# A squared-ReLU MLP whose second pass over W_down opens with the last pair, then takes the last but one by seven products

## The chip, the cores and the metric

The kernel runs on one core of one Trainium2 chip. The metric is the device time of one execution in microseconds (us): the median of three runs of the kernel before is 2126.35 us (2126.24 to 2127.57). One more execution was taken with the hardware profiler; all rows shown are from it.

## The reference, cut to what matters

Two layers, each a mixer (attention and a gated short convolution, one shared output projection) followed by an MLP. Everything is float32, x has 256 rows and 2048 columns, and the MLP is 8192 wide:

```python
D_MODEL = 2048
SEQ = 256
DEPTH = 2
D_FF = 4 * D_MODEL
...
        hm = _rmsnorm(x, mlp_norm_g[l]) @ w_up[l]
        x = x + jnp.square(jax.nn.relu(hm)) @ w_down[l]
```

The change touches only the second of these lines, the product with W_down (8192 x 2048).

## The kernel before, in words

**Float32 by three products.** Every operand is split into a rounded part ("h", "hi") and the rest ("l", "lo"). One product of two operands is three matmuls (`TERMS`): hi with hi, hi with lo, lo with hi. The rounding to hi is ScalarE's (ACT) work, the subtraction for lo VectorE's (DVE). TensorE (PE) does the matmuls, each 128x128 weights against 128x512 moving values here. In the MLP the activations are PE's weights and the rows of W_down the moving side.

**Pairs.** The width of 8192 is cut into `NP` = 32 pairs, numbered 0 to 31, of 256 hidden columns each: pair i is 256 columns of W_up and the 256 rows of W_down that they meet. A pair against one half (1024 columns) of W_down is a 2x2 by 2x2 block product. Done in the ordinary way it is 8 block products, 24 matmuls (`OWN`, line 1354 in the second pass, line 1267 in the first). Done "by seven" it is Strassen's scheme in Winograd's form: 7 block products, 21 matmuls (helper `product`, line 1177).

**Forms.** Seven products need sums on both sides. Those of the activations (`S1` to `S4`) are made once per pair by `square`; a pair's hi and lo of the eight blocks A21, A11, A22, A12, S1 to S4 are one tile `f` (helper `rounded`). Those of the W_down rows are made per pair and half by `quarters` in three jobs: `plain` (the blocks b1 and b2: b1h, b1l, b2h, b2l), `sums` (t[0:2] at line 1019, then t13h, t13l, then t[2] at line 1022 and t[3] at line 1023) and `more` (t24h, t24l). The seven products use them in that order: products 1, 2, 3 from b1 and b2, then 5 and 7 from t13, then 6 and 4 from t24. Ordinary rows only need hi and lo (`whi`, line 325, and `wlo`, line 326; two halves per pair).

**Two passes.** The first pass runs over pairs 0 to 31: it makes a pair's activations from W_up (the matmuls of `upc`, line 1128) and, two pairs later (`LAG`), multiplies them with the left half of W_down; pairs 0 to 30 by seven, pair 31 in the ordinary way. The sums of the left half lie in eight banks of PSUM (tiles `pr`), and are drained into x at the pass's end by one ACT and eight DVE instructions of 128x512 (lines 1237 and 1232). The second pass multiplies all pairs with the right half (banks `rt`), in an order of its own, written out by hand:

```python
ORDER = tuple(i % NP for i in range(NP - LAG, 2 * NP - LAG))
SEVEN = ORDER[3:NP - LAG:2]
ORDINARY = tuple(i for i in ORDER if i not in SEVEN)
PLAIN = ORDINARY[LAG:]
```

So before, the order is 30, 31, 0, 1, 2, ... 29. Pairs 30 and 31 still have their tiles `f` in SBUF; they come first and in the ordinary way. Of the others, the odd ones from 1 to 27 go by seven; their tiles were stored in DRAM (`whole`) during the first pass and are fetched again by `load_again` on the POOL queue, 896 KB each, two turns ahead. The even ones, 28 and 29 go in the ordinary way and are fetched as `g` from `plain`, two pairs to a block. Rows of W_down come on the SP queue: for pairs by seven into one of three rooms named `draw`, for ordinary pairs into one of three buffers `raw`.

**What sets the order.** PE's instructions stand in the order in which the program writes them. ACT and DVE instructions are placed by a scheduler with a time model of its own, within limits that the code sets (`late` keeps an instruction in program order, `behind` puts it after another); each engine then executes its list strictly in that order. Which weight job is made after which is the list `made_in`, with the table `slots` that says behind which ordinary half the three jobs of a pair by seven are written; a job is written at most three (`AHEAD`) ahead of its use. hi and lo of ordinary rows have three buffers each, so a `whi` waits until PE has finished the half three before it.

Of the kernel before, what the change touches and what calls it, by code (L numbers as in the profile page):

```python
# [10 lines left out]
F32R = mybir.dt.float32r  # L11
# [4 lines left out]
P = 128  # L16
# [16 lines left out]
AHEAD = 3  # L33
NP = DFF // (2 * P)
LAG = 2
ORDER = tuple(i % NP for i in range(NP - LAG, 2 * NP - LAG))
SEVEN = ORDER[3:NP - LAG:2]
ORDINARY = tuple(i for i in ORDER if i not in SEVEN)
PLAIN = ORDINARY[LAG:]

OUT_JOBS = D // P // 2 * (D // CH)
EARLY_UP = {(0, 0): 15, (0, 1): 17, (1, 0): 23}
# [70 lines left out]
def trunk(ctx: ExitStack, tc: tile.TileContext, x, w_in, w_out, conv_w, q_norm_g, k_norm_g,  # L113
# [10 lines left out]
    dram = ctx.enter_context(tc.tile_pool(name="dram", bufs=1, space=bass.MemoryType.DRAM))  # L124
# [808 lines left out]
    def mlp(l, mnorm, ahead, last):  # L933
# [3 lines left out]
        with ExitStack() as scope:  # L937
            upool = scope.enter_context(tc.tile_pool(name="upool", bufs=3))
            fpool = scope.enter_context(tc.tile_pool(name="fpool", bufs=2))
# [16 lines left out]
            raws, forms, units_made, drains = {}, {}, [], []  # L956
# [22 lines left out]
            def load_rows(i, col):  # L979
                raw = (upool.tile([P, 2, 2 * CH], F32, tag="uraw", name="raw") if col and i not in SEVEN else  # L980
                       tile_of("draw", [P, 2, 2 * CH], F32, (first, "draw"), (second, "draw1"),
# [7 lines left out]
            def quarters(i, col=0):  # L989


                keep = late if i == SEVEN[0] and col else lambda ins: None

# [78 lines left out]

            whole = {i: dram.tile([P, 2, 7, P], F32R, name=f"whole{l}_{i}") for i in SEVEN}
            plain = [dram.tile([P, 2, 2, 4, P], F32R, name=f"plain{l}_{b}")
                     for b in range(len(PLAIN) // 2)]
            again, unit_loads = {}, []
# [3 lines left out]
                    unit_loads.append(nc.gpsimd.dma_start(dst, src))  # L1082

            def load_again(i):
                again[i] = fpool.tile([P, 2, 8, P], F32R, tag="f", name="f")
                load_unit(again[i][:, :, 1:], whole[i])

            base = len(weights.jobs)
            where = {}
            for i in ORDER:  # L1090
                where[i] = len(weights.jobs)
                if i in SEVEN:
                    weights.jobs += quarters(i, 2 * CH)
# [5 lines left out]
            mine = [where[i] + k for i in ORDINARY for k in range(2)]  # L1099
            slots = {}  # L1100
            for i in SEVEN:
                before = [j for j in mine if j < where[i]][-4:] if i != SEVEN[0] else [
                    mine[0], mine[1], mine[4]]
                js = [where[i] + k for k in range(3)]
                if len(before) == 4 and SEVEN.index(i) and where[SEVEN[SEVEN.index(i) - 1]] > before[0]:
                    before = [before[2], before[2], before[3]]
                for j, b in zip(js, before):
                    slots.setdefault(b, []).append(j)
# [32 lines left out]
            def square(i, h):  # L1141


                u = h[:, 0:4].rearrange("p a c -> p (a c)")
                nc.scalar.activation(u, u, AF.Relu)
                top = h[:, 0:4].rearrange("p (k t) c -> p k t c", t=2)[:, :, 0]
                nc.vector.tensor_mul(top, top,
                                     mnorm.ratio.unsqueeze(1).to_broadcast([P, 2, P]))
                nc.scalar.activation(u, u, AF.Square)
                if i < NP - 1:  # L1150
                    nc.vector.tensor_add(h[:, S1], h[:, A21], h[:, A22])
                    nc.vector.tensor_sub(h[:, S2], h[:, S1], h[:, A11])
                    nc.vector.tensor_sub(h[:, S3], h[:, A11], h[:, A21])
                    nc.vector.tensor_sub(h[:, S4], h[:, A12], h[:, S2])
                if i in SEVEN:
                    f = rounded(h, 1, 8)
                    nc.gpsimd.dma_start(whole[i], f[:, :, 1:])
                    return f
                f = rounded(h, 0, 8 if i < NP - 1 else 4)
                if i in PLAIN:  # L1160
                    b = PLAIN.index(i)
                    stored.append(nc.gpsimd.dma_start(plain[b // 2][:, b % 2], f[:, :, :4]))
                return f

            def rounded(h, lo, hi):
                f = fpool.tile([P, 2, 8, P], F32R, tag="f", name="f")
                units_made.append((
                    nc.scalar.activation(f[:, 0, lo:hi], h[:, lo:hi], AF.Copy),
                    nc.vector.tensor_sub(f[:, 1, lo:hi], h[:, lo:hi], f[:, 0, lo:hi].bitcast(F32))))
                return f  # L1170
# [9 lines left out]
            fs = {}  # L1180
# [66 lines left out]
            f = fs[NP - 2]  # L1247
# [15 lines left out]
            for k in range(2):  # L1263
                b = weights.take()
# [24 lines left out]
            for n in (5, 4, 8):  # L1289
                prods[n] = bank(f"rt{l}{n}")  # L1290
            for i in ORDER:
                if i in SEVEN:
                    f = again[i]
                    one, end = i == SEVEN[0], i == SEVEN[-1]
                    if one:
                        w2 = mm.tile([P, 2, CH], F32, tag="mm2", name=f"rt{l}1")
                        prods[1], prods[6] = w2[:, 0], w2[:, 1]
                        prods[7] = ps.tile([P, CH], F32, tag="av", name=f"rt{l}7", bufs=1)
                    b11, b21, b22 = weights.take()
                    product(1, f, A11, b11, one, end)  # L1300
                    product(2, f, A12, b21, False)
                    product(3, f, S4, b22, False)
                    work.tick()
                    t1, t3 = weights.take()
                    product(5, f, S1, t1, one, end)
                    product(7, f, S3, t3, one, end)
                    work.tick()
                    t2, t4 = weights.take()
                    product(6, f, S2, t2, one, end)
                    product(4, f, A22, t4, False)  # L1310
                    work.tick()
                    if end:
                        for dst, v in shared(*right):
                            nc.vector.tensor_add(dst, dst, v)
                        if not last:
                            spare = (prods[7], prods[5])
                            work.start(norm.chunk(0, 2, spare), 2)
                            work.start(norm.chunk(1, 2, spare), 6)
                    continue
                n = ORDINARY.index(i)  # L1320
                if NP // 2 - 6 <= n and sums:
                    finish_left()
                if 0 < n <= len(SEVEN):
                    load_again(SEVEN[n - 1])
                b, slot = divmod(n - LAG, 2)
                if b < 0:
                    own = lambda k, t, pa: fs[i][:, pa, 2 * k + t]
                else:
# [3 lines left out]
                    if slot == 1 and b + 2 < len(plain):  # L1332
                        block(b + 2)
                if i == ORDER[-1]:
                    both = [weights.take() for k in range(2)]
# [14 lines left out]
                for k in range(2):  # L1350
                    w = weights.take()
                    for n, t, p in OWN:
                        for m, (pa, pw) in enumerate(TERMS):
                            nc.tensor.matmul(  # L1354
                                prods[p], own(k, t, pa), w[pw][:, n],
                                start=(i == ORDER[0] and k == 0 and m == 0), stop=False)
                        if t:
# [47 lines left out]
```

## Time and profile before

| what | value |
|---|---|
| median of three runs | 2126.35 us |
| the profiled execution | 2126.2 us, its span 2124.1 us |
| PE busy | 2118.3 us of the span |
| DVE busy | 1738.9 us |
| ACT busy | 1299.0 us |
| granted TensorE clock | 1.0 |
| HBM traffic | 234 GB/s over the span |

The span is what the profiler's records cover; the 2.1 us that the execution is longer lie around it. Matmuls overlap in the records: one is shown as about 0.39 us long, and the next begins before it ends. How long PE takes for each is read from the starts. An answer of the timeline gives the start in us, the length in us, the engine, the line, the operation, the tiles and, in brackets, how long the engine had been idle and what released it; "x2" is two instructions in one row. Layer 0's first pass ends and its second begins at 899.69 us of the span, layer 1's at 1954.93 us.

### The profile page before, as it was taken

Reading aid. Unit: us, or ns where it says so; the run is one execution under the profiler, and the core shown is the slowest. Engines: PE = TensorE matmul, PEld = TensorE weight load, DVE = VectorE, ACT = ScalarE, POOL = GpSimd, SP = SyncE. Lnnn points to the kernel's source line nnn. Section 1 sums busy time; section 2 is a strip of 40 time slices with the busy share of each in tenths; the row PEclk is TensorE's granted clock in tenths of the full one; section 3 lists DMA queues with packets and bytes.
Section 4 is the critical chain, followed back from the end, with each engine's and each line's share of the span. In section 5 each row is a group of like instructions: output and inputs, shape, how many; then the busy total and the mean of one; then the engine's idle time right before and its main releaser. Section 6 shows DMA issues by size and latency. Waiting matters only on the chain.

```text
span 2124.1 us, 28896 instructions
## 1 busy us (share of the span) xinstructions
PE 2118.3 (100%) x10926; PEld 1804.4 (85%) x10926; DVE 1738.9 (82%) x2397; ACT 1299.0 (61%) x1775; POOL 188.7 (9%) x282
## 2 busy tenths in 40 slices
PE   9999999999999999999999999999999999999999
PEld 7888888888888888888888888888888888888887
DVE  6677688788888888899866776887888888888897
ACT  6556456666666666655565664566666666666553
POOL 3021200000000000011011221000000000000110
PEclk9999999999999999999999999999999999999999
DMA  8655567687787777699666556677778778776994
GB/s 262 188 165 162 186 210 249 207 251 242 244 244 243 244 245 242 222 360 345 219 215 178 158 163 194 213 247 220 238 246 250 235 245 249 237 245 212 385 359 156
DMA packets 293322, 497.99 MB, mean 234 GB/s; under 512 B 10723, under 2 KB 191541, under 8 KB 293184
## 3 DMA queue, kind: packets, MB, share of 16 engines
q1 hardware_dynamic: 263056, 406.88, 60.1%
q0 software_dynamic: 30080, 89.26, 13.0%
q8 instruction: 85, 1.39, 0.3%
q14 instruction: 53, 0.43, 0.1%
q10 hardware_dynamic: 48, 0.02, 0.0%
HBM read 451.53 MB, written 44.59 MB: 234 GB/s over the span
## 4 chain that ended last, share of the span: by engine, by line
PE 99%; DVE 0%; DMA 0%; ACT 0%; issue 0%
PE upc L1128 31%; PE pr L1177 14%; PE rt L1354 8%; PE rt L1177 6%; PE ci L479 4%; PE gc L479 4%; PE gb L479 4%; PE k L457 4%; PE v L457 4%; PE q L457 4%; PE o L457 4%; PE o L875 3%; PE o L893 1%; PE upw L1128 1%; PE up L1128 1%; PE sc L654 1%
## 5 line engine op out<-in xcount | busy, mean ns | idle before, releaser
L325 ACT ACTIVATE whi<-raw 128x1024 fp32r<-128x1024 f32 x308 | 326.4, 1060 | 411.7 <-PE rt L1354 137.5
L326 DVE TENSOR_TENSOR wlo<-raw,whi 128x1024 fp32r<-128x1024 f32 x308 | 379.5, 1234 | 196.1 <-ACT whi L325 191.1
L1128 PE MATMUL upc<-nT,uhi 128*128 128x512 f32 x1920 | 477.6, 391 | 0.0
L974 ACT ACTIVATE uhi<-uraw 128x1024 fp32r<-128x1024 f32 x256 | 270.4, 1057 | 261.5 <-PE upc L1128 237.3
L1128 PEld LDWEIGHTS upc<-nT,uhi 128*128 128x128 f32 x1920 | 352.9, 188 | 68.0
L975 DVE TENSOR_TENSOR ulo<-uraw,uhi 128x1024 fp32r<-128x1024 f32 x256 | 313.1, 1223 | 118.6 <-ACT uhi L974 109.4
L1128 PEld LDWEIGHTS upc<-nT,ulo 128*128 128x128 f32 x1920 | 262.0, 191 | 18.7
L1128 PE MATMUL upc<-nT,ulo 128*128 128x256 f32 x1920 | 267.8, 283 | 0.0
L1354 PE MATMUL rt<-whi,g 128*128 128x512 f32 x480 | 153.0, 389 | 0.0
L1002 DVE TENSOR_TENSOR t13l<-t,t13h 128x1024 fp32r<-128x1024 f32 x90 | 110.0, 1222 | 2.1
L1019 DVE TENSOR_TENSOR t<-draw 128x1024 f32<-128x1024 f32 x90 | 109.8, 1220 | 0.8
L1002 DVE TENSOR_TENSOR b2l<-draw,b2h 128x1024 fp32r<-128x1024 f32 x90 | 109.6, 1218 | 0.4 <-ACT b2h L1000 0.4
L1002 DVE TENSOR_TENSOR t24l<-t,t24h 128x1024 fp32r<-128x1024 f32 x90 | 109.6, 1218 | 0.0
L1354 PEld LDWEIGHTS rt<-whi,g 128*128 128x128 f32 x480 | 90.1, 188 | 18.6
L1000 ACT ACTIVATE t13h<-t 128x1024 fp32r<-128x1024 f32 x90 | 95.8, 1064 | 3.3 <-PE rt L1177 0.6
L1177 PE MATMUL pr<-t13h,f 128*128 128x512 f32 x248 | 96.6, 391 | 0.0
L1000 ACT ACTIVATE t24h<-t 128x1024 fp32r<-128x1024 f32 x90 | 94.5, 1050 | 1.0 <-DVE t L1023 1.0
L1000 ACT ACTIVATE b2h<-draw 128x1024 fp32r<-128x1024 f32 x90 | 94.5, 1050 | 0.9 <-PE pr L1177 0.8
L1354 PE MATMUL rt<-wlo,g 128*128 128x512 f32 x240 | 93.4, 389 | 0.0
L1177 PE MATMUL pr<-b2h,f 128*128 128x512 f32 x248 | 86.8, 391 | 0.0
L1177 PE MATMUL pr<-t24h,f 128*128 128x512 f32 x248 | 86.8, 391 | 0.0
L457 PE MATMUL k<-whi,nT 128*128 128x512 f32 x256 | 86.1, 400 | 0.0
(414 smaller groups left out, 4086.7 us busy)
## 6 DMA issues: line engine op xcount, KB each, us to landing
uraw<-in_w_up_dram SPq DMA_DIRECT2D x128, 1024.0 KB, 5.9
raw<-in_w_in_dram SPq DMA_DIRECT2D x190, 512.0 KB, 3.9
draw<-in_w_down_dram SPq DMA_DIRECT2D x92, 1024.0 KB, 6.5
raw<-in_w_down_dram SPq DMA_DIRECT2D x36, 1024.0 KB, 8.1
raw<-in_w_out_dram SPq DMA_DIRECT2D x52, 512.0 KB, 4.7
whole<-f POOLq DMA_DIRECT2D x28, 896.0 KB, 4.5
f<-whole POOLq DMA_DIRECT2D x28, 896.0 KB, 8.7
plain<-f POOLq DMA_DIRECT2D x32, 512.0 KB, 3.8
```

Of the source, the lines that this page charges most:

```text
L325: self.splits.append((nc.scalar.activation(hi, raw, AF.Copy), nc.vector.tensor_sub(lo, raw, hi.bitcast(F32))))
L326: nc.vector.tensor_sub(lo, raw, hi.bitcast(F32))))
L457: nc.tensor.matmul(acc[:, t], a.ap[:, pa, k % KG, t * P:(t + 1) * P], (hi, lo)[pw][:, j], start=(k == 0 and n == 0), stop=(k == nk - 1 and ...
L479: nc.tensor.matmul(acc[:, f, 0] if part else acc[:, f], wt[:, k % 4, fs], a.ap[:, 0, k % KG] if part else a.ap[:, :, k % KG], start=(part ...
L974: nc.scalar.activation(hi, src, AF.Copy)
L975: nc.vector.tensor_sub(lo, src, hi.bitcast(F32))
L1000: keep(nc.scalar.activation(hi, src, AF.Copy))
L1002: keep(nc.vector.tensor_sub(lo, src, hi.bitcast(F32)))
L1019: keep(nc.vector.tensor_sub(t[:, 0:2], raw[:, :, 1], raw[:, 0]))
L1128: nc.tensor.matmul(acc[:, 0] if part else acc, wt[:, k], a.ap[:, 0, k % KG] if part else a.ap[:, :, k % KG], start=(part == 0 and kh == 0 ...
L1177: nc.tensor.matmul(prods[n], f[:, pa, a], b[pw], start=(start and m == 0), stop=(stop and m == 2))
L1354: nc.tensor.matmul(prods[p], own(k, t, pa), w[pw][:, n], start=(i == ORDER[0] and k == 0 and m == 0), stop=False)
```

## The change

The second pass's order becomes 31, 30, 0, 1, 2, ... 29. Pair 31 stays ordinary. Pair 30 becomes the first of the pairs by seven, and its products read the tile `f` that is still in SBUF (`fs[i]`), so it isn't stored in DRAM or fetched. The table `slots` gives pair 30's three jobs their places: the first two behind pair 31's first half, the third behind its second (before, pair 1 was the first by seven, with its jobs behind pair 30's first and second half and pair 0's first). The two buffers of tiles `f`, before one rotating tag "f", become two tags "f0" and "f1" that are taken in turns by a count of the pairs, and `load_again` is called for pairs 1 and 3 at pair 0 and then one per ordinary pair.

```diff
@@ -33,10 +33,10 @@
-ORDER = tuple(i % NP for i in range(NP - LAG, 2 * NP - LAG))
-SEVEN = ORDER[3:NP - LAG:2]
+ORDER = (NP - 1, NP - 2, *range(NP - 2))
+SEVEN = ORDER[1:NP - LAG:2]
 ORDINARY = tuple(i for i in ORDER if i not in SEVEN)
-PLAIN = ORDINARY[LAG:]
+PLAIN = ORDINARY[1:]
@@ -1072,7 +1072,7 @@
-            whole = {i: dram.tile([P, 2, 7, P], F32R, name=f"whole{l}_{i}") for i in SEVEN}
+            whole = {i: dram.tile([P, 2, 7, P], F32R, name=f"whole{l}_{i}") for i in SEVEN[1:]}
@@ -1082,7 +1082,7 @@
             def load_again(i):
-                again[i] = fpool.tile([P, 2, 8, P], F32R, tag="f", name="f")
+                again[i] = fpool.tile([P, 2, 8, P], F32R, tag=f"f{SEVEN.index(i) % 2}", name="f", bufs=1)
                 load_unit(again[i][:, :, 1:], whole[i])
@@ -1100,7 +1100,7 @@
             for i in SEVEN:
                 before = [j for j in mine if j < where[i]][-4:] if i != SEVEN[0] else [
-                    mine[0], mine[1], mine[4]]
+                    mine[0], mine[0], mine[1]]
@@ -1152,7 +1152,7 @@
-                if i in SEVEN:
+                if i in SEVEN[1:]:
                     f = rounded(h, 1, 8)
                     nc.gpsimd.dma_start(whole[i], f[:, :, 1:])
                     return f
@@ -1163,7 +1163,7 @@
             def rounded(h, lo, hi):
-                f = fpool.tile([P, 2, 8, P], F32R, tag="f", name="f")
+                f = fpool.tile([P, 2, 8, P], F32R, tag=f"f{len(units_made) % 2}", name="f", bufs=1)
@@ -1290,7 +1290,7 @@
                 if i in SEVEN:
-                    f = again[i]
+                    f = again[i] if i in again else fs[i]
@@ -1320,9 +1320,9 @@
-                if 0 < n <= len(SEVEN):
-                    load_again(SEVEN[n - 1])
-                b, slot = divmod(n - LAG, 2)
+                for s in (1, 2) if n == 1 else (n + 1,) if 1 < n < len(SEVEN) - 1 else ():
+                    load_again(SEVEN[s])
+                b, slot = divmod(n - 1, 2)
```

What this makes of the instructions at the boundary of the passes (layer 0; layer 1's rows are the same but for the numbers). On DVE, from the last forms made before the left half is drained: `e` and `x` with `pr` are the drains, `draw_8531` are the W_down rows of the first pair by seven (pair 1 before, pair 30 after), `raw_8525` those of the second pass's first ordinary pair. (The numbers at the tiles are each build's own: the same number need not be the same tile in both.) Before:

```order
L1002 TENSOR_TENSOR b2l_8538<-draw_8531,b2h_8537 128x1024
L1232 SCALAR_TENSOR_TENSOR e2_8558<-pr01_4147,rowf2_3903,e1_8557 128x512
L1232 SCALAR_TENSOR_TENSOR e4_8560<-pr05_4150,rowf2_3903,e2_8558 128x512
L1232 SCALAR_TENSOR_TENSOR x1_84<-pr05_4150,rowf2_3903,x1_84 128x512
L1232 SCALAR_TENSOR_TENSOR e3_8559<-pr07_4151,rowf2_3903,e2_8558 128x512
L326 TENSOR_TENSOR wlo_8548<-raw_8525,whi_8547 128x1024
L1232 SCALAR_TENSOR_TENSOR x0_83<-pr04_4149,rowf2_3903,x0_83 128x512
L1232 SCALAR_TENSOR_TENSOR x0_83<-pr02_4148,rowf2_3903,x0_83 128x512
L1232 SCALAR_TENSOR_TENSOR x1_84<-pr02_4148,rowf2_3903,x1_84 128x512
L1232 SCALAR_TENSOR_TENSOR x1_84<-pr08_8566,rowf2_3903,x1_84 128x512
```

After:

```order
L1002 TENSOR_TENSOR b2l_8538<-draw_8531,b2h_8537 128x1024
L1019 TENSOR_TENSOR t_8547<-draw_8531 128x1024
L1232 SCALAR_TENSOR_TENSOR e2_8562<-pr01_4147,rowf2_3903,e1_8561 128x512
L1232 SCALAR_TENSOR_TENSOR e4_8564<-pr05_4150,rowf2_3903,e2_8562 128x512
L1232 SCALAR_TENSOR_TENSOR x1_84<-pr05_4150,rowf2_3903,x1_84 128x512
L1232 SCALAR_TENSOR_TENSOR e3_8563<-pr07_4151,rowf2_3903,e2_8562 128x512
L1002 TENSOR_TENSOR t13l_8550<-t_8547,t13h_8549 128x1024
L1022 TENSOR_TENSOR t_8547<-t_8547,draw_8531 128x512
L1232 SCALAR_TENSOR_TENSOR x0_83<-pr04_4149,rowf2_3903,x0_83 128x512
L326 TENSOR_TENSOR wlo_8604<-raw_8525,whi_8603 128x1024
L1232 SCALAR_TENSOR_TENSOR x0_83<-pr02_4148,rowf2_3903,x0_83 128x512
L1232 SCALAR_TENSOR_TENSOR x1_84<-pr02_4148,rowf2_3903,x1_84 128x512
```

Three DVE instructions of the first pair by seven (t[0:2], t13l, t[2]) now stand among the drains, ahead of the second half's `wlo` of the first ordinary pair. DVE's list goes on, before:

```order
L1019 TENSOR_TENSOR t_8599<-draw_8531 128x1024
L1002 TENSOR_TENSOR b1l_8707<-draw_8704,b1h_8706 128x512
L326 TENSOR_TENSOR wlo_8622<-raw_8619,whi_8621 128x1024
L326 TENSOR_TENSOR wlo_8626<-raw_8619,whi_8625 128x1024
L1002 TENSOR_TENSOR t13l_8602<-t_8599,t13h_8601 128x1024
L1022 TENSOR_TENSOR t_8599<-t_8599,draw_8531 128x512
L326 TENSOR_TENSOR wlo_8646<-raw_8643,whi_8645 128x1024
L1023 TENSOR_TENSOR t_8599<-draw_8531,t_8599 128x512
L326 TENSOR_TENSOR wlo_8666<-raw_8643,whi_8665 128x1024
L1002 TENSOR_TENSOR t24l_8650<-t_8599,t24h_8649 128x1024
```

After:

```order
L1232 SCALAR_TENSOR_TENSOR x1_84<-pr08_8570,rowf2_3903,x1_84 128x512
L1002 TENSOR_TENSOR b1l_8632<-draw_8629,b1h_8631 128x512
L326 TENSOR_TENSOR wlo_8626<-raw_8623,whi_8625 128x1024
L1023 TENSOR_TENSOR t_8547<-draw_8531,t_8547 128x512
L326 TENSOR_TENSOR wlo_8690<-raw_8623,whi_8689 128x1024
L326 TENSOR_TENSOR wlo_8712<-raw_8709,whi_8711 128x1024
L1002 TENSOR_TENSOR b1l_8718<-draw_8715,b1h_8717 128x512
L1002 TENSOR_TENSOR t24l_8620<-t_8547,t24h_8619 128x1024
```

The last form of the first pair by seven, t24l, now stands behind three `wlo` (pair 0's two halves in `raw_8623`, pair 2's first in `raw_8709`) and two `b1l` (pairs 1 and 3). On PE, the second pass's second pair was, before (pair 31, second half, its start):

```order
L1354 MATMUL rt02_8595<-whi_8625,f_8485 128x512
L1354 MATMUL rt02_8595<-wlo_8626,f_8485 128x512
L1354 MATMUL rt02_8595<-whi_8625,f_8485 128x512
L1354 MATMUL rt04_8597<-whi_8625,f_8485 128x512
L1354 MATMUL rt04_8597<-wlo_8626,f_8485 128x512
L1354 MATMUL rt04_8597<-whi_8625,f_8485 128x512
```

and is after (pair 30, products 6 and 4, and the start of pair 0):

```order
L1177 MATMUL rt01_8651<-t24h_8619,f_8339 128x512
L1177 MATMUL rt01_8651<-t24l_8620,f_8339 128x512
L1177 MATMUL rt01_8651<-t24h_8619,f_8339 128x512
L1177 MATMUL rt04_8601<-t24h_8619,f_8339 128x512
L1177 MATMUL rt04_8601<-t24l_8620,f_8339 128x512
L1177 MATMUL rt04_8601<-t24h_8619,f_8339 128x512
L1354 MATMUL rt02_8599<-whi_8625,g_8501 128x512
```

Pair 30's last two products read t24 in the second of the pass's pairs; before, the first t24 of the second pass was read in its fourth pair. In each layer PE has 3 matmuls fewer.

## The prediction

> **What bounds the kernel now.** The first view is the page, then PE's waits, then the granted clock of the page's 40 slices:
>
> ```profile
> PE 2118.3 (100%) x10926; PEld 1804.4 (85%) x10926; DVE 1738.9 (82%) x2397; ACT 1299.0 (61%) x1775; POOL 188.7 (9%) x282
> PEclk9999999999999999999999999999999999999999
> PE warm L170 <- DVE ones L162: 1.0, 1, 1.0
> PE q L457 <- DVE wlo L347: 0.4, 2, 0.2
> PE gps L181 <- DMA ngv<-in_attn_norm_g_dram: 0.2, 1, 0.2
> ```
>
> PE is busy for 2118.3 of 2124.1 us, and the three rows are all its waits in the trace, all at the kernel's start. So nothing can be won by an earlier operand: the time falls by the matmuls that go, and rises by every wait that appears on PE. A PE wait is lost for good, since no later wait is there to absorb it.
>
> The price of one matmul comes from the chain of waits around layer 0's second pass (start, length, what; both pieces without a gap):
>
> ```profile
> 899.85 16.32 PE rt L1354 x72
> 916.17 4.76 PE rt L1177 x21
> ```
>
> 72 ordinary matmuls in 16.32 us and 21 of a pair by seven in 4.76 us are 0.2267 us each in both. So a pair by seven takes 4.76 us against 5.44 us for an ordinary one. PE's timeline shows where the pass begins and when a pair by seven wants its t24 (starts in us, first pair by seven before):
>
> ```profile
> 899.69 0.39 PE L1354 MATMUL rt<-whi,f 128*128 128x512 f32 x1
> ...
> 916.01 0.39 PE L1177 MATMUL rt<-b1h,f 128*128 128x512 f32 x1
> ...
> 919.63 0.39 PE L1177 MATMUL rt<-t24l,f 128*128 128x512 f32 x1
> ```
>
> t24l is first read 3.62 us after the pair's start (16 matmuls).
>
> **The part that is removed.** Per layer, 24 matmuls become 21: 3 x 0.2267 = 0.68 us, over two layers 1.36 us, 0.06% of the span. That is the whole possible gain. No transfer goes: 14 tiles `whole` and 16 `plain` are stored and fetched as before, and W_down is read once. DVE gets five rows more per layer and ACT two (pair 30's forms, seven and four, in place of two `wlo` and two `whi`), which is free only where PE doesn't come to wait for them.
>
> **The part that is moved.** Pair 30's forms must be ready one pair after the pass's start, where before the first pair by seven came three pairs after it. PE's times in the changed kernel, if nothing waits: pair 31 from 899.69 to 899.69 + 5.44 = 905.13; pair 30's t24l wanted at 905.13 + 3.62 = 908.75; pair 0 from 909.89. DVE's timeline of before at this place gives both its state and the price of every row:
>
> ```profile
> 893.81 1.23 DVE L1002 TENSOR_TENSOR b2l<-draw,b2h 128x1024 fp32r<-128x1024 f32 x1 [0.18 <-ACT b2h L1000]
> 894.95 1.53 DVE L1232 SCALAR_TENSOR_TENSOR e<-pr,rowf,e 128x512 f32<-128x512 f32 x2
> 896.40 0.74 DVE L1232 SCALAR_TENSOR_TENSOR x<-pr,rowf,x 128x512 f32<-128x512 f32 x1
> 897.06 0.74 DVE L1232 SCALAR_TENSOR_TENSOR e<-pr,rowf,e 128x512 f32<-128x512 f32 x1
> 898.26 1.23 DVE L326 TENSOR_TENSOR wlo<-raw,whi 128x1024 fp32r<-128x1024 f32 x1 [0.46 <-ACT whi L325]
> 899.40 2.72 DVE L1232 SCALAR_TENSOR_TENSOR x<-pr,rowf,x 128x512 f32<-128x512 f32 x4
> 902.04 1.21 DVE L1019 TENSOR_TENSOR t<-draw 128x1024 f32<-128x1024 f32 x1
> 903.17 0.68 DVE L1002 TENSOR_TENSOR b1l<-draw,b1h 128x512 fp32r<-128x512 f32 x1
> 903.77 2.35 DVE L326 TENSOR_TENSOR wlo<-raw,whi 128x1024 fp32r<-128x1024 f32 x2
> 906.05 1.22 DVE L1002 TENSOR_TENSOR t13l<-t,t13h 128x1024 fp32r<-128x1024 f32 x1
> ...
> 910.73 1.23 DVE L1002 TENSOR_TENSOR t24l<-t,t24h 128x1024 fp32r<-128x1024 f32 x1
> ```
>
> Prices are differences of starts, since rows overlap: 1.14 us for a 128x1024 subtraction (893.81 to 894.95), 0.60 for a 128x512 one (903.17 to 903.77), 1.45 for the first two drains (894.95 to 896.40), 0.66 for each further drain (2.64 for four). Before, t24l was done at 911.96 for a use at 919.63, with 7.7 us to spare. And DVE is full here: in this row of the windows (PE, PEld, DVE, ACT, POOL) it is busy for all of 10.90 us.
>
> ```profile
> 899.70:910.60 10.90, 10.90 (x50) 9.03 (x49) 10.90 (x13) 6.17 (x6) 0.70 (x1) 1.00 0.64 200
> ```
>
> Now DVE's new list from 894.95 on, where b2l of the first pair by seven is done as before: t[0:2] 1.14 (896.09); two drains 1.45, two more 1.32 (898.86); t13l 1.14, t[2] 0.60, a drain 0.66 (901.26); the `wlo` of pair 31's second half 1.14 (902.40); three drains 1.98 (904.38); b1l 0.60, `wlo` of pair 0 1.14, t[3] 0.60 (906.72); two `wlo` 2.28 (909.00); b1l 0.60 (909.60); then t24l, done 1.22 later, at **910.82**. The sum ahead of it is six long rows (6.84), four short ones (2.40), eight drains (5.41): 14.65 us from 894.95.
>
> Does something other than DVE hold a row of it? ACT's timeline:
>
> ```profile
> 897.17 1.06 ACT L325 ACTIVATE whi<-raw 128x1024 fp32r<-128x1024 f32 x1 [2.19 <-PE pr L1267]
> 899.89 1.06 ACT L325 ACTIVATE whi<-raw 128x1024 fp32r<-128x1024 f32 x1 [1.66 <-PE pr L1267]
> 902.61 1.06 ACT L325 ACTIVATE whi<-raw 128x1024 fp32r<-128x1024 f32 x1 [1.66 <-PE rt L1354]
> 905.38 1.06 ACT L325 ACTIVATE whi<-raw 128x1024 fp32r<-128x1024 f32 x1 [0.76 <-ACT t13h L1000]
> ```
>
> A `whi` follows 0.2 us behind the end of the half that frees its buffer (the half ends at 902.41, it starts at 902.61). Pair 2's first `whi`, new ahead of t24h in ACT's list, waits for the end of pair 31, 905.13: done at 906.4, where DVE wants it at 907.86; t24h, behind t[3] (906.8), is done at 907.9, where DVE wants it at 909.60. So DVE alone sets t24l.
>
> The wait that follows, from PE's first waits on a `wlo` (DVE's rows, then PE's):
>
> ```profile
> 9.90 0.69 DVE L347 TENSOR_TENSOR wlo<-raw,whi 128x512 fp32r<-128x512 f32 x1
> ...
> 9.83 0.63 PE L457 MATMUL q<-whi,nT 128*128 128x512 f32 x2
> 10.64 0.50 PE L457 MATMUL q<-wlo,nT 128*128 128x512 f32 x1 [0.18 <-DVE wlo L347]
> 10.98 0.63 PE L457 MATMUL q<-whi,nT 128*128 128x512 f32 x2
> ```
>
> The lo is done at 10.59; the matmul on it starts 0.05 later, and the next 0.34 after that in place of 0.23. So PE would start the matmul on t24l at 910.87 in place of 908.75 (2.12 us) and lose another 0.11 on restarting: **2.23 us per layer**. Bounds: nothing, if t24l were in time; and 2.6 us, if three rows of the list each start 0.12 us late, as t[2] does where it reads what DVE has just written (1.26 us behind, in place of 1.14):
>
> ```profile
> 922.57 1.22 DVE L1019 TENSOR_TENSOR t<-draw 128x1024 f32<-128x1024 f32 x1
> 923.83 0.69 DVE L1022 TENSOR_TENSOR t<-t,draw 128x512 f32<-128x512 f32 x1
> ```
>
> I take 2.23, since in the new list other rows stand between.
>
> What else the change adds lies under other work. Pair 31's second `wlo` ends at 902.49 for a use at 899.69 + 13 x 0.2267 = 902.64: just in time, and if it is 0.1 late the loss is part of the 2.23, since t24l's time is DVE's own. The banks of products 1 and 7 are those of the last drains (904.4), used from 905.13 and 907.85. After t24l DVE's next rows (b2l, t[0:2], t[2], t[3], t13l, t24l of pair 1) end at about 916.6, and pair 1 starts at 909.89 + 2.23 + 5.44 = 917.56.
>
> SP's next load, into the buffer of pair 31's rows, goes out once its `wlo` is done: at 902.5, where before it was 899.52:
>
> ```profile
> 899.52 7.01 SPq L984 DMA_DIRECT2D raw<-in_w_down_dram  x2
> ```
>
> Queued behind it are the rows of pairs 5 and 6. This one is for pair 4, which PE reaches after 927.7 (917.56 + 4.76 + 5.44), so 3 us are covered. POOL's fetch of pair 1's tile is in the rivals.
>
> Layer 1 stands alike: the drains begin at 1950.19 and the pass at 1954.93, 4.74 us apart as 894.95 and 899.69 are:
>
> ```profile
> 1950.19 1.53 DVE L1232 SCALAR_TENSOR_TENSOR e<-pr,rowf,e 128x512 f32<-128x512 f32 x2
> 1954.93 0.39 PE L1354 MATMUL rt<-whi,f 128*128 128x512 f32 x1
> ```
>
> **The sum.** Per layer -0.68 + 2.23 = +1.55 us, twice +3.1 us. On the profiled execution's own 2126.2 us (span 2124.1 and 2.1 around it) that is **2129.3 us**; against the median of the runs, 2126.35, 0.14% more. A measurement of this kernel can tell about 0.2% from no change, 4.25 us: 2122.1 to 2130.6 counts as the same.
>
> **Rivals.**
>
> *No wait: the three matmuls are all that happens.* For it: DVE idles a little at the boundary (0.18 us before 893.81, 0.46 before 898.26), and t24l had 7.7 us to spare. Against: the new list puts 14.65 us of work between 894.95 and t24l, and nothing of it can start much earlier, since the drains wait for PE's last products. 2126.2 - 1.36 = 2124.8 us. Chance 0.10, with what lies between it and the forecast.
>
> *The tile of pair 1 lands late (slower).* It is fetched into the buffer that pair 31 leaves at 905.13, POOL's queue has nothing ahead of it, and PE wants it at 917.56. Before, the same fetch went out at 905.60 under a DVE as busy:
>
> ```profile
> 905.60 0.70 POOL L1082 DMA_DIRECT2D f<-whole  x1 [19.72 <-PE rt L1354]
> DMA to landing us min/median/max: 6.7/6.7/6.7
> ```
>
> It took 6.7 us: here, 912.3, 5 us early. It decides from a landing of 12.0 us on. The slowest load of rows between 860 and 930 took 13.0 us:
>
> ```profile
> DMA to landing us min/median/max: 5.0/6.7/13.0
> ```
>
> At 13.0 PE would wait until 918.6, 1.0 us per layer and 0.11 for the restart, 2.2 us over both: 2131.5, slower by 0.24%. The later loads on SP now start closer to this fetch (902.5 and about 907), which speaks for it. Chance 0.07. [...]
>
> *The wait closes the clock (slower).* Rows: the granted clock is 9 in all slices, the first too, where PE waited 1.0 us at once; no idle as long as 2 us is in the trace. If the clock fell to half for the matmuls left of pair 30 and the next pair (4 + 24 at 0.2267 more), that is 6.3 us per layer, 2142 us. Chance 0.03. [...]
>
> *The wait is longer than worked out,* since ACT or a transfer holds a row of DVE's list that I take as free: beyond 2.8 us per layer it shows as slower (2 x 2.8 - 1.36 = 4.25). Chance 0.06, about 2131.5.
>
> **How the numbers follow.** Forecast 0.74 (a wait of 1.9 to 2.6 us gives 2128.6 to 2130.0; with the runs' own spread, 0.6 us more on either side), no wait or less of it 0.10, the rest 0.16. The range 2127.0 to 2131.2 takes in the forecast, a wait of 1.1 us, and most of the late fetch up to a landing of 12.8 us. Same: forecast and no wait, 0.84, of which I give 0.02 to faster, though that needs 4.25 us where 1.36 are there: 0.82. Slower: 0.16.
>
> **What would show it.** In the changed profile PE's waits should have a new row, PE rt on DVE t24l (line 1002), twice, about 2.0 to 2.2 us each, at about 908.9 and 1965.7; t24l should start near 909.6; PE's rows fall by 6 matmuls; the pass should leave pair 30 near 912.1 where two pairs ended at 910.57. A PE wait on `f` at pair 1 would show the second rival, a granted clock below 1.0 the third, and no row at all the first. The forecast is wrong if t24l starts before 908 or if PE waits at any other place.

## The result: 0.3% slower, with a lower clock behind the wait

The changed kernel takes 2132.65 us (median of 10 runs, 2131.05 to 2133.11), the kernel before, timed beside it, 2126.31 us (10 runs, 2126.24 to 2127.73): ratio 1.0027, 95% interval 1.0019 to 1.0035. The forecast was 2129.3 us, with a range up to 2131.2.

The median hides levels: three runs stand at 2131.05 to 2131.13, seven at 2132.5 to 2133.1. The profiled execution took 2131.13 us and is one of the lower ones; the rows of this section are from it. Its page begins:

```profile
PE 2119.2 (100%) x10920; PEld 1803.1 (85%) x10920; DVE 1746.6 (82%) x2407; ACT 1303.0 (61%) x1779; POOL 189.0 (9%) x282
PEclk9999999999999999999999999999999999999999
```

PE has 6 matmuls fewer (10926 before) and yet 0.9 us more of busy time. PE's waits, with the new row first:

```profile
PE rt L1177 <- DVE t24l L1002: 3.8, 2, 1.9
PE warm L170 <- DVE ones L162: 1.0, 1, 1.0
PE q L457 <- DVE wlo L347: 0.4, 2, 0.2
```

Layer 0 on the timeline, first DVE, then PE (start and length in us, idle time before and its releaser in brackets):

```profile
906.77 2.36 DVE L326 TENSOR_TENSOR wlo<-raw,whi 128x1024 fp32r<-128x1024 f32 x2
909.04 0.69 DVE L1002 TENSOR_TENSOR b1l<-draw,b1h 128x512 fp32r<-128x512 f32 x1
909.64 1.23 DVE L1002 TENSOR_TENSOR t24l<-t,t24h 128x1024 fp32r<-128x1024 f32 x1
```

```profile
908.63 0.39 PE L1177 MATMUL rt<-t24h,f 128*128 128x512 f32 x1
910.92 0.50 PE L1177 MATMUL rt<-t24l,f 128*128 128x512 f32 x1 [1.90 <-DVE t24l L1002]
911.25 0.63 PE L1177 MATMUL rt<-t24h,f 128*128 128x512 f32 x2
911.72 0.39 PE L1177 MATMUL rt<-t24l,f 128*128 128x512 f32 x1
911.95 0.40 PE L1177 MATMUL rt<-t24h,f 128*128 128x512 f32 x1
912.18 0.39 PE L1354 MATMUL rt<-whi,g 128*128 128x512 f32 x1
```

This is the forecast wait, nearly to the row: t24l starts at 909.64 (909.60 foretold), PE goes on at 910.92 (910.87), and pair 30 is left at 912.18 (912.1). Layer 1 has the same wait, and then something that layer 0 has not:

```profile
1965.43 0.39 PE L1177 MATMUL rt<-t24h,f 128*128 128x512 f32 x1
1967.71 0.50 PE L1177 MATMUL rt<-t24l,f 128*128 128x512 f32 x1 [1.89 <-DVE t24l L1002]
1968.05 0.74 PE L1177 MATMUL rt<-t24h,f 128*128 128x512 f32 x2
1968.59 0.63 PE L1177 MATMUL rt<-t24l,f 128*128 128x512 f32 x1
1969.02 0.63 PE L1177 MATMUL rt<-t24h,f 128*128 128x512 f32 x1
1969.44 0.63 PE L1354 MATMUL rt<-whi,g 128*128 128x512 f32 x1
...
1971.15 0.63 PE L1354 MATMUL rt<-wlo,g 128*128 128x512 f32 x1
1971.58 0.75 PE L1354 MATMUL rt<-whi,g 128*128 128x512 f32 x2
1972.17 0.40 PE L1354 MATMUL rt<-wlo,g 128*128 128x512 f32 x1
```

From 1968.59 on a matmul comes every 0.43 us in place of 0.23. The windows view, one row for a stretch of time, names the cause in its third column from the end, the granted clock:

```profile
899.70:930.00 30.30, 28.40 (x125) 23.09 (x125) 30.09 (x34) 16.23 (x18) 4.31 (x7) 1.00 0.90 317
1956.00:1986.00 30.00, 28.11 (x117) 22.62 (x116) 29.58 (x33) 14.34 (x15) 4.30 (x7) 0.94 0.86 298
1970.00:1971.40 1.40, 1.40 (x5) 1.11 (x4) 1.37 (x3) 1.06 (x1) 1.40 (x3) 0.50 1.00 395
```

The clock fell to half behind the wait in layer 1 and not in layer 0. The page's row of 40 slices, 53 us each, can't show it: all 9.

The clock record of the trace gives the stretches of each granted clock. Here it is for seven profiles, in us from the span's start: when the full clock first opens (is first granted), and each half-clock stretch up to the last matmul. The kernels e3 to e12 are those of the experiments below.

```
profile             us       full from   half from (length)
before            2126.24       6.20     none
after             2131.13       5.77     1968.43 (3.413)
e5_again          2131.06       5.25     1967.91 (3.413)
e11_after_again   2132.42      10.12     1969.37 (3.413)
e12_after_again   2130.41       9.26     none
e3_longer_wait    2131.73       5.82     none
e9_longer_again   2134.60       4.90     912.84 (3.413), 1970.98 (3.413)
```

Every stretch between two changes is a whole multiple of 3.413 us, full ones too (1962.664 = 575 x 3.413 in after): the clock changes on a grid, whose place differs from one execution to the next (the first opening, a point of it, lies at 4.90 to 10.12 us in the seven). One piece of it, 3.413 us long, is called a window here, and a fall to half clock a closing. At half clock, where the starts are 0.4267 us apart (seven such steps from 1968.59 to 1971.58), a window does 3.413 / 0.4267 = 8 matmuls in place of 3.413 / 0.2267 = 15, so one closing costs 3.413 - 8 x 0.2267 = 1.6 us. In after: 2126.2 + 3.1 (the forecast's sum) + 1.6 = 2130.9, measured 2131.13.

### The profile page after: what moved, and what is told of

The parts are those of the page before. It is cut to its first block, busy times and chain, and to the rows that moved or that the text cites. A ratio compares the mean times of both kernels' runs of the same rounds, so it can differ in the third digit from the quotient of the medians.

```text
span 2128.9 us, 28900 instructions
## 1 busy us (share of the span) xinstructions
PE 2119.2 (100%) x10920; PEld 1803.1 (85%) x10920; DVE 1746.6 (82%) x2407; ACT 1303.0 (61%) x1779; POOL 189.0 (9%) x282
## 5 line engine op out<-in xcount | busy, mean ns | idle before, releaser
L326 DVE TENSOR_TENSOR wlo<-raw,whi 128x1024 fp32r<-128x1024 f32 x304 | 374.0, 1232 | 194.9 <-ACT whi L325 190.0
```

Source lines behind the costliest of these rows:

```text
L326: nc.vector.tensor_sub(lo, raw, hi.bitcast(F32))))
```

## The experiments

Theory A is that the change costs its wait on t24l and what the clock does behind it; the rivals are the two buffers of the tiles `f` with their fetch, another cost of the new order, and an upper level of the times that has nothing to do with the wait.

**e1: the order of the forms freed.** The forms of pair 30's right half, on ACT and on DVE, are no longer held in program order, so that the scheduler may place t24l earlier. Tables, buffers and PE's order stay as changed.

```diff
-                keep = late if i == SEVEN[0] and col else lambda ins: None
+                keep = lambda ins: ins
```

> The changed kernel, but the scheduler may place the forms of the first pair by seven (pair 30) freely on ACT and DVE: t24l then stands right behind the left half's drains, ahead of the three wlo and two b1l that held it. Nothing else differs. By DVE's prices t24l is done at about 904, where PE wants it at 908.8. Theory A (the whole loss is the wait for t24l, 2.24 us per layer, and the halved clock that follows it, 1.65 us where it follows): no PE wait at t24l, granted clock 1.000 in every run, 2126.3 - 1.36 = 2124.9 us. Theory B (something behind the wait is late too, in the fetches or in DVE's list, and the clock is only a by-product): over 2126.3.

Measured 2124.93 us (11 runs, 2124.59 to 2126.36) beside 2126.23 for before (27 runs, shared with e2 to e4): 0.9994, interval 0.9984 to 1.0003. DVE's timeline of e1:

```profile
901.11 2.72 DVE L1232 SCALAR_TENSOR_TENSOR x<-pr,rowf,x 128x512 f32<-128x512 f32 x4
903.75 1.21 DVE L1002 TENSOR_TENSOR t24l<-t,t24h 128x1024 fp32r<-128x1024 f32 x1
904.88 0.68 DVE L1002 TENSOR_TENSOR b1l<-draw,b1h 128x512 fp32r<-128x512 f32 x1
905.48 2.35 DVE L326 TENSOR_TENSOR wlo<-raw,whi 128x1024 fp32r<-128x1024 f32 x2
```

t24l stands right behind the last drain and is done at 904.96, 4.2 us before PE reads it at 909.14; the rows that stood ahead of it follow. No wait on it is left, the mean granted clock is 1.000 in every run, and the difference of the medians, -1.30 us, is the -1.36 of the six matmuls. So all that the change loses, it loses by the order that is held; in after, DVE's rows stand without a gap ahead of t24l and PE waits for no form of ACT's, so it is DVE's part of it that counts. This version lies ahead of both kernels by its median, but its interval reaches 1.0003, so against before it isn't shown to be faster.

**e2 and e6: the gap filled.** Product 7 of pair 30 is followed by spare matmuls into product 6's bank, which product 6 then starts afresh: 9 in e2, which fill the wait, and 2 in e6, which leave half of it.

```diff
+                    for _ in range(FILL if one else 0):
+                        nc.tensor.matmul(prods[6], f[:, 0, S2], b11[0], start=True, stop=True)
```

> The changed kernel with 9 more matmuls of 128x512 per layer ahead of pair 30's product 6 (into product 6's bank, which product 6 then starts anew, so the result is the same): PE is busy while t24l is late. The scheduler now puts one b1l behind t24l, so t24l is done at 910.2; PE reaches its matmul at 908.75 + 9 x 0.227 = 910.8. Per layer -0.68 + 2.04. Theory A: no wait, clock 1.000 in every run, 2126.3 + 2.7 = 2129.0 us, so 3.6 us less than the changed kernel though PE comes to the next pair 0.1 us earlier only. Theory B (lateness behind the wait, not the clock): as the changed kernel, 2131 to 2133.

> The changed kernel with 2 more matmuls per layer ahead of product 6 (its bank is then started anew, the result is the same). The scheduler puts a b1l behind t24l, so t24l is done at 910.2 and PE wants it at 909.2: the wait is 1.07 us in place of 2.14. Without a halved clock 2126.25 + 2 x (1.52 + 0.11 - 0.68) = 2128.15 us. Theory A: half a wait closes the clock seldom or never, the level at 2128.15 holds most runs. If any restart closed it as often as the wait of 2.1 us does: most runs at 2129.8 and 2131.4.

e2 took 2129.31 us (11 runs, 2128.86 to 2130.63; 1.0016, interval 1.0007 to 1.0025). PE does 18 matmuls that are of no use, and still e2 stands only 3.1 us above its before, where the changed kernel stands 6.3 (first timing) and 4.7 us (e5) above its own. e6 took 2128.65 us (11 runs, 2128.12 to 2129.90; 1.0012, 1.0003 to 1.0020), with this wait, and no half clock behind it:

```profile
PE rt L1178 <- DVE t24l L1003: 1.7, 2, 0.9
```

Seven of its runs stand at 2128.1 to 2128.7, near the 2128.15 that was expected; four are at 2129.6 to 2129.9, and the profile, one of those, shows why, at the kernel's start:

```profile
6.24 0.79 PE L458 MATMUL q<-whi,nT 128*128 128x512 f32 x1
...
8.41 0.63 PE L458 MATMUL q<-wlo,nT 128*128 128x512 f32 x1
8.84 0.63 PE L458 MATMUL q<-whi,nT 128*128 128x512 f32 x1
9.27 1.01 PE L558 MATMUL tpb<-ident,x 128*128 128x128 f32 x4
9.97 0.54 PE L458 MATMUL q<-whi,nT 128*128 128x512 f32 x1
10.35 0.40 PE L458 MATMUL q<-wlo,nT 128*128 128x512 f32 x1
```

The clock first opened at 10.1 us there, where nine of the fourteen profiles open it at 4.9 to 7.8, and the first matmuls ran at half speed: some 1.4 us. The profile of e2 is another such execution: it took 2130.63 us, opened at 10.2 and has neither a wait on t24l nor a half clock up to its last matmul. A level of this height stands in before's runs too (2127.3 to 2128.0 in 6 of 48), so the change doesn't make it; that a late opening makes it there as well is likely, but none of those six has a profile. e2 has two more runs as high, 2130.42 and 2130.58, with a mean granted clock of 0.999 where 1.000 was expected in every run; where they lost their time stays open.

**e3: a longer wait.** One more 128x1024 subtraction ahead of t24h in DVE's list (t[0:2] written again, which nothing reads after it).

```diff
+                    if i == SEVEN[0] and col:
+                        raw = forms["raw"]
+                        keep(nc.vector.tensor_sub(forms["t"][:, 0:2], raw[:, :, 1], raw[:, 0]))
```

> The changed kernel with one more DVE instruction of 128x1024 per layer (t[0:2] made a second time, with the same values) ahead of t24l: the wait grows from 2.1 to about 3.3 us. Theory A: the same with +1.14 us per layer, and the clock halved in every layer of every run, not in 17 of 20: 2129.4 + 2.3 + 3.3 = 2135.0 us, with no run at 2133.3 or below. If the time at half clock grew with the wait, above 2136. Theory B gives 2132.7 + 2.3 = 2135.0 too, with both levels still there.

Measured 2133.23 us (5 runs: 2131.73, 2133.11, 2133.23, 2133.64, 2133.65; 1.0032, 1.0019 to 1.0045). A miss, and the most useful one: the profiled run, at 2131.73, has PE idle for 3.04 us in place of 1.90, in both layers, and its clock stays full.

```profile
911.97 0.50 PE L1180 MATMUL rt<-t24l,f 128*128 128x512 f32 x1 [3.04 <-DVE t24l L1002]
912.31 0.63 PE L1180 MATMUL rt<-t24h,f 128*128 128x512 f32 x2
912.77 0.39 PE L1180 MATMUL rt<-t24l,f 128*128 128x512 f32 x1
```

So the length of a wait alone doesn't decide. What is left is where it lies on the grid.

**e4: one rotating tag for the tiles `f` again.** e1 with the old naming of their two buffers.

```diff
-                again[i] = fpool.tile([P, 2, 8, P], F32R, tag=f"f{SEVEN.index(i) % 2}", name="f", bufs=1)
+                again[i] = fpool.tile([P, 2, 8, P], F32R, tag="f", name="f")
-                f = fpool.tile([P, 2, 8, P], F32R, tag=f"f{len(units_made) % 2}", name="f", bufs=1)
+                f = fpool.tile([P, 2, 8, P], F32R, tag="f", name="f")
```

> The kernel of the free order (no wait at t24l), with the tiles f on the one rotating tag as before the change. The first tile fetched in the second pass then goes into pair 30's buffer, not pair 31's, and leaves POOL when pair 30 ends, at about 910.4; before, such a fetch took 6.5 to 10.8 us: it lands at 917 to 921, where PE wants it at 915.3. Theory A for any cause of a wait: a PE wait on f of 1.7 to 5.8 us per layer, and behind it the halved clock: 2124.9 + 3.6 to 11.8 + 3.3, that is 2132 to 2140 us. If only waits on DVE closed the clock: 2128.5 to 2136.7 with the clock at 1.000. If the names of the buffers don't matter: 2124.9.

Measured 2125.06 us (11 runs, 2124.72 to 2126.33; 0.9995, 0.9987 to 1.0004), as e1; no wait on f. A miss: I expected the rotation to hand out pair 30's buffer first, and it hands out pair 31's, as the names do:

```profile
905.65 0.70 POOL L1082 DMA_DIRECT2D f<-whole  x1 [19.72 <-PE rt L1354]
910.41 0.72 POOL L1082 DMA_DIRECT2D f<-whole  x1 [4.05 <-PE rt L1177]
```

The naming of the buffers neither costs nor brings anything.

**e7 and e8: many waits of many lengths.** To e1 two (e7) or four (e8) more such subtractions are added for every pair by seven of the right half, again on t[0:2], which nothing reads after them.

```diff
+                    if col:
+                        raw = forms["raw"]
+                        for _ in range(2):
+                            nc.vector.tensor_sub(forms["t"][:, 0:2], raw[:, :, 1], raw[:, 0])
```

> The kernel of the free order, with t[0:2] made twice more (same values) in every pair by seven of the second pass, 30 pairs in all. DVE then has 11.2 us of work for each two pairs of 10.2 us and becomes the bound, so PE waits in almost every pair by seven, about 1 us each: some 28 waits in one profile, each with its length and the granted clock behind it. Time about 2125 + 28 x 1.0 = 2153 us. Theory A: few or none of these waits, all under 1.7 us, have a halved clock behind them. If any restart closes the clock, most have.

> As the last, with t[0:2] made four times more: 13.5 us of DVE work for each two pairs of PE's 10.2, PE waits 3.2 us per two pairs, in one piece or in two. Time about 2125 + 28 x 3.2 = 2215 us. Theory A: waits of 2 to 3.3 us in one piece are followed by a halved clock for about 3.4 us in most cases, and the share grows with the length of the wait. If the share doesn't grow with the wait (as the 3.0 us waits without one in the longer-wait run suggest), length alone doesn't decide.

One run each: 2169.9 and 2241.6 us, 17 and 27 us over what was expected. The waits aren't the reason: PE's waits in the second passes add up to 27.0 us in e7 and 66.3 in e8, where 28 and 90 were expected, though some are for ACT's forms (the second row below). What was left out is the half clock: by the starts, the matmuls at half clock take some 11 us more in e7 and 34 in e8. The waits of e7:

```profile
PE rt L1181 <- DVE t24l L1002: 15.8, 9, 2.6
PE rt L1181 <- ACT t24h L1000: 8.8, 6, 4.1
PE rt L1181 <- DVE t13l L1002: 2.4, 1, 2.4
```

The clock records of the two show 7 and 15 half-clock stretches. In the next table the grid of each record is laid over PE's starts, and PE's idle time is added up in each window of the second passes, in these two profiles and in those of after, e3, e5, e6 and e9 to e12. Idle time runs from the end of one matmul to the next one's start; a matmul counts as 0.2267 us, one on which PE goes on after a wait as 0.34, and gaps under 0.05 us are left out. The windows at full clock with over 0.3 us of it:

```
PE idle in the grid window     windows     clock of the next window
0.4 to 1.85 us                   43        full in all
1.90 and 1.94 us                  2        half after 1.90, full after 1.94
1.97 to 3.29 us                  26        half in all
```

All 27 half-clock stretches of these profiles stand behind such a window. That 1.90 us closed the clock and 1.94 didn't shows that this sum is good to about 0.05 us, or isn't quite what decides. Of the 27 stretches 17 last one window; where waits follow each other, one in e7 and eight in e8 last two, and one in e8 four.

**e5, e9 to e12: the same kernels again, for the grid and the levels.** e5, e11 and e12 are the changed kernel, e9 and e10 are e3.

> The changed kernel once more, on the chip and beside the runs of the kernel before that the next three have. The wait is 2.1 us in each layer. Theory A (the clock falls to half where a stretch of about 3.4 us, placed anyhow against the wait, holds enough idle time; 1.65 us each time): levels at 2129.4, 2131.0 and 2132.7 us for none, one or two layers, each level with its share; in the first timing two layers came in 7 of 10. Theory C (it is a matter of the chip or of the moment, not of the wait): all runs at one level, 2129.4.

> The changed kernel with the longer wait of 3.0 us, once more, for its profile. Its earlier runs stood at 2131.7 us (one) and at 2133.1 to 2133.7 (four). Theory A (a grid of 3.413 us whose place differs between executions): where the profile is at the upper level, one of the two waits leaves 1.9 us or more idle in one grid window and a half-clock window of 3.413 us follows it; at 2131.7 both waits are split by a grid line with less than 1.9 us on either side. Theory B (the upper level is nothing but a late first opening of the clock, about 10 us after the start, worth 1.4 us, and a wait of 3.0 us never closes it): the profile shows the late opening and no half clock at 912 or 1970.

> A third profile of the kernel with the 3.0 us wait. Theory A: every half-clock window stands behind a grid window with 1.9 us idle or more, and none behind one with 1.8 us or less; time 2131.7 us plus 1.4 to 1.9 for each such window, plus 1.4 if the clock opens late. Theory B: no half clock behind a wait at all; time 2131.7 or 2133.1.

> The changed kernel itself, for a third profile. Its runs stand at 2129.3, 2131.0 and 2132.7 us. Theory A: 2129.3 with both waits split by a grid line, 2131.0 with one of two layers closed, 2132.7 with both closed. Theory B (the upper level is one closing and a late first opening): at 2132.4 or more the profile shows the clock open at about 10 us and one half-clock window.

> A fourth profile of the changed kernel, for the same question: 2129.3, 2131.0 or 2132.7 us with no, one or two half-clock windows behind the waits (theory A), or the upper level with one such window and a first opening at about 10 us (theory B).

e5, on another chip than e1 to e4: 2131.01 us (11 runs, 2129.27 to 2132.76) beside 2126.36 (21 runs, shared with e6 to e8): 1.0022, interval 1.0013 to 1.0031. One run at 2129.27 and one at 2130.55 (mean granted clock 1.000), seven at 2130.9 to 2131.1 (0.999), two at 2132.6 and 2132.8 (0.998). The others took 2134.60 (e9), 2131.72 (e10), 2132.42 (e11) and 2130.41 us (e12), beside 2126.75. How their waits lie on the grid (idle us in the one or two windows that a wait touches, and the clock behind it):

```
profile            layer 0             layer 1
after              1.44 + 0.62 full    2.05 half
e5_again           0.99 + 1.08 full    2.07 half
e11_after_again    0.93 + 1.11 full    2.04 half
e12_after_again    0.42 + 1.63 full    1.75 + 0.3 full
e3_longer_wait     1.58 + 1.62 full    1.77 + 1.41 full
e10_longer_again   1.33 + 1.85 full    1.55 + 1.65 full
e9_longer_again    0.74 + 2.47 half    2.76 + 0.42 half
```

The grid decides in all fourteen. The same wait of 3.0 us that left the clock full in e3 and e10 closed it twice in e9:

```profile
911.90 0.50 PE L1180 MATMUL rt<-t24l,f 128*128 128x512 f32 x1 [3.04 <-DVE t24l L1002]
912.24 0.62 PE L1180 MATMUL rt<-t24h,f 128*128 128x512 f32 x2
912.70 0.49 PE L1180 MATMUL rt<-t24l,f 128*128 128x512 f32 x1
913.00 0.63 PE L1180 MATMUL rt<-t24h,f 128*128 128x512 f32 x1
913.42 0.63 PE L1357 MATMUL rt<-whi,g 128*128 128x512 f32 x1
913.85 0.63 PE L1357 MATMUL rt<-wlo,g 128*128 128x512 f32 x1
```

and e9 is 2.9 us longer than e10 for it; it isn't twice 1.6 because 0.42 us of layer 1's wait lies in the half-clock window itself.

Theory B, that the upper level is only the late opening, falls with e9, but half of it stands: e11 reached 2132.42 with one closing and an opening at 10.12 us, and e12 2130.41 with none and an opening at 9.26. So a run near 2132.5 can be made in two ways, by two closings (2126.3 + 3.1 + 3.2 = 2132.6) or by one and a late opening (2132.4). The mean clock, which is on record for every run, tells them apart. It leaves out what lies ahead of the first opening (e6, open at 10.10 us, has 1.000) and counts the half clock behind the last matmul up to the span's end. One closing takes 0.0008 off it, that end at most 0.0005 (2.1 us in e2, the longest of the fourteen profiles). So one closing leaves 0.999, as in e11, and it takes two for 0.998, as in e9. Six of the first timing's seven upper runs have 0.998 and by this had two closings, though no profile of the changed kernel shows two; the seventh, 2132.57, has 0.999 and fits e11. The four upper runs of e3 have 0.999, so none of them closed twice; whether each lost its 1.4 to 1.9 us by one closing or by a late opening stays open.

## Why the prediction was wrong

**What held.** The sum of the change itself, +1.55 us per layer: t24l 0.04 us from its foretold start, PE's resumption 0.05, the same in layer 1, and a matmul after the wait 0.33 us behind it for 0.34. From the pass's start to the end of pair 30 PE takes 12.42 us (899.76 to 912.18) for 45 matmuls that need 10.20, so the wait and the restart cost 2.22 us where 2.23 was foretold. The run of e5 with full clock throughout stands at 2129.27 us where 2129.3 was foretold, and the kernel without the wait at 2124.93 (e1) for 2124.8 or 2124.9. DVE alone set t24l, as said: PE shows no wait on t24h, on pair 31's second `wlo`, on SP's rows for pair 4, or on `f`. The second rival, a tile of pair 1 that lands late, didn't come: its fetch went out under a full DVE in 0.71 us, and pair 1 began without a wait at 917.63 (917.56 foretold).

**What failed: the rival "the wait closes the clock".** The forecast's sum has nothing for it, and its chance, 0.03, and its price, 6.3 us per layer, were both wrong. The runs show none, one or two closings of 1.6 us each on top of the sum, and by the mean clock two in six of the ten runs that were timed first.

The chance rested on rows that could not carry it. "No idle as long as 2 us is in the trace" would say only that nothing was tried there, not that the clock bears it. The wait at the kernel's start was no test either: the clock hadn't opened yet (6.20 us in before, where that wait ends at 1.04), and a slice of 53 us shows a 9 all the same. And the trace does hold a longer idle time, behind the last matmul, which starts at 2119.61 us. Its grid window runs from 2119.05 to 2122.46, and PE is idle for 2.6 us of it. The windows view of before has the granted clock in that stretch and behind it, third from the end:

```profile
2119.05:2122.45 3.40, 0.95 (x5) 0.45 (x3) 1.13 (x2) 0.00 (x0) 0.00 (x0) 1.00 0.58 221
2122.46:2124.10 1.64, 0.00 (x0) 0.00 (x0) 0.00 (x0) 0.00 (x0) 0.00 (x0) 0.50 0.00 0
```

So the clock falls to half behind a window that isn't idle as a whole, in the very trace that the prediction read.

That a wait of 2.2 us leaves the clock full, as the forecast's sum has it, was the author's estimate, and the runs don't show it: 1.97 us of idle time within a window of the grid, 3.413 us long, closed the clock each time, 1.85 never. By that, a wait of 2.05 us closes the clock where it lies, but for some 0.15 us, in one window.

The price assumed that half clock lasts through pair 30 and the next pair, 28 matmuls. In this kernel it lasted one window: 8 matmuls, 1.6 us. The rival at 2129.3 + 1.6 or + 3.2 would have stood at 2130.9 and 2132.5, and with the chance that it deserved the range would have had to reach beyond that.

**What chance it deserved** can be worked out from the grid, with 1.9 us as the edge. Let PE's idle time of 2.05 us begin s us into a window in layer 0. The clock closes there for s up to 3.41 - 1.9 = 1.5 (enough of the wait lies in that window), and from 3.41 - 0.15 = 3.26 on (enough lies in the next), half of all places. In after, layer 1's wait begins 1056.80 us after layer 0's (1965.43 less 908.63), 309 windows and 2.1 us; a closing in layer 0 adds 1.6. So if layer 0 closes, layer 1 begins at s + 0.3 and closes too for s up to 1.2; if not, it begins at s + 2.1, and closes for s from 1.5 to about 2.8; from there to 3.26 neither does. If all places were alike, an estimate: both layers closed in some 40% of the executions, one in 47%, none in 13%. The profiles agree: s is 1.97, 2.42 and 2.48 in after, e5 and e11, which closed in layer 1 alone, and 3.00 in e12, which closed in none. By the times and mean clocks of the 21 runs of the first timing and e5, 8 closed in both layers, 11 in one and 2 in none. That the places are evenly spread isn't shown.

The median moves with this, too: 2132.65 in the first timing and 2131.01 in e5 are the same kernel with another share of the levels. On which level a median lands is, by the grid, luck: e5's would have lain inside the range, and the prediction would have been no better for it.

## What to carry to other kernels

A wait of about 2 us on a TensorE that is otherwise packed can cost nearly twice its length: here 2.2 us for the wait and 1.6 for one window at half clock behind it. Look for it in narrow windows of the granted clock and in the time from one matmul's start to the next behind the wait, since wide slices hide it (the 53 us ones of after all show 9); and where such a wait can't be removed, even work of no use in it can be cheaper, as in e2 (3.1 us above its before, where the changed kernel stood 6.3 and 4.7). When an order is held by hand for one set of operations and they are then wanted earlier, ask again whether it should be held: here that one line was the whole loss.

## What was not expected of the hardware

In these profiles the granted clock changes on a grid of 3.413 us, whose place differs between executions of one kernel (the stretch at half clock begins at 1968.43 us in after, 1967.91 in e5, 1969.37 in e11). It fell to half behind each of the 26 windows in which PE was idle for 1.97 us or more, and behind none of the 43 with 1.85 or less, so that a wait of 3.04 us that a grid line cut near its middle (e3, e10) left the clock full and one of 2.05 us within a window didn't. In e8 the clock came back after half-clock windows with up to 0.67 us of idle time, and stayed half after those with 0.67 or more: to the hundredth, this sum doesn't tell them apart.

When the full clock first opens varies from 4.9 to 10.6 us after the start in the fourteen profiles. In e6 and e2 an opening at 10.1 or 10.2 us goes with a time some 1.4 us above the lower level.
